# Convolutions beside the sampled steps, early scale constants, and a mixer start in another order, in a two-layer streaming encoder on one core

## The chip, the cores and the metric

One core of a Trainium2 chip. The metric is the device time of one execution in microseconds (us), the median over the runs shown. Of the core's engines TensorE (PE) does the matmuls, VectorE (DVE), ScalarE (ACT) and GpSimd (POOL) the rest, and SyncE (SP) issues most of the transfers.

## What is computed

One inference step of a two-layer encoder over 512 prompt tokens and 8 sampled sequences of 16 tokens, 640 tokens in all, 1024 wide, in fp32. Each layer is a SwiGLU, a mixer, and a second SwiGLU, each between two RMS norms with a modulation per sequence:

```python
h = _rmsnorm(x, norm_g[l, 2]) * (1.0 + sc2) + sh2
y, states = _token_mixer(h, l, layer_past, w_in, b_if, conv_w, conv_b, lam, ...)
x = x + g2 * _rmsnorm(y, norm_g[l, 3])
...
z = h @ w_in[l]                                   # 1024 -> 5640 columns
lmb = jnp.exp(jnp.sum(lp[0] * lp[1])) - jnp.exp(jnp.sum(lp[2] * lp[3])) + lam_init
...
a = p[:, :, 0] - lmb * p[:, :, 1]                 # differential attention, 4 heads
...
qk, conv_new = _causal_conv(z[..., OFF_MQ:OFF_MV], conv0, conv_w[l], conv_b[l])   # width 4, 1024 channels
qk = jax.nn.silu(qk)
...
hm, (c_new, n_new, m_new) = _mlstm(qm, km, vm, log_i, log_f, c0, n0, m0, blk)
merged = g[..., :D_MODEL] * (o_a @ w_pa[l]) + g[..., D_MODEL:] * (o_m @ w_pb[l])
```

The prompt attends within itself; every sampled sequence attends to 256 cached rows and its own 16. `z` feeds attention q, k, v, the memory's q and k (through the convolution), v, output gate, input and forget gates, and the two branch gates.

## The kernel before

Every fp32 matmul is made of three on reduced-precision parts (`three`; line 91 issues them, line 80 those into a PSUM bank that two tiles share): an operand is split into a high and a low part (`split`, lines 298 and 299; `split_to`, lines 504 and 505), the cast on ACT, the remainder on DVE or POOL. The 640 tokens are held transposed, as 8 groups of 128 channels, in two halves of 320 tokens.

A layer runs first FFN, mixer, second FFN. Large projections are computed in blocks (`blocks`, from line 740): a 2x2 block product with 7 products of 12 matmuls in place of 8. For it the token halves are combined (`combine`, lines 517 to 520: DVE and POOL alternate in place on the rows that `pre_norm` made, after they have been split) into t1 to t4, and the weight blocks are summed on POOL (lines 757, 758, 764, 771) before each sum is split on ACT and DVE (`split_to`, W tiles, four slots). A product lands in a PSUM tile (`acc`, four), from which DVE adds it into K tiles (line 747) or into the caller's `put` (line 887).

The mixer's order is written out in Python, and the program's scheduler moves instructions within what dependencies, buffers and its own estimates allow:

1. `attn_columns` (L876 in `first_columns`): q and k of heads 0 and 1, first for token half 0, then for token half 1; then `attn_values(0)`, which takes the values of both heads from five tiles of 128 tokens (`natural`, k0 in two slabs), and `head_rows`.
2. `side_blocks`: 14 blocks (q and k of heads 2 and 3, then the two branch gates, then the memory's q and k inputs, spilled to `pre` in DRAM), each interleaved through `zip_longest` with one part of the 16 prompt steps and 8 sampled steps of the attention. A sampled step loads 256 cached key rows (X tile), transposes them on PE (line 1110), scores (bank from X and S), takes a softmax on ACT and DVE (lines 1120 to 1132, `dm` and `sm` tiles), and multiplies with the cached values.
3. `history`, `values(0)`, `conv(0)`, `values(1)`, `conv(4)`. A `conv` call handles four groups of 128 channels: load the projection from `pre`, then on DVE a scale (line 1210), three multiply-adds (line 1212) each for the 512 prompt tokens (128x512) and for the sampled ones (128x128, from the tile `dm`, copied at line 1203), and a last multiply with the SiLU's tanh (line 1215).
4. `attention_out`, the memory's gates and chunks, the branches, the output projection.

At the mixer's start DVE also makes the scale constants from lambda: a load, two multiply-reduces (line 855), an Exp on ACT (857, with a table load), and five small operations (859 to 866, a memset on POOL among them).

SBUF tiles have few slots: W 4, X 3 (cached keys and, in the mixer's blocks, the sums s1 and s2 in one X tile), Fv 5, raw 4, C 8, S 42.

## Time and profile before

| | |
|---|---|
| median of 3 runs | 3140.17 us (3135.35 to 3141.33) |
| profiled execution, its own time | 3134.3 us |
| its span on the core | 3132.6 us |
| PE busy | 2989.2 us, 95% of the span |
| DVE busy | 2200.2 us, 70% |
| ACT, POOL busy | 1423.6 us, 1211.8 us |
| mean granted TensorE clock | 0.985 of 2.4 GHz |

How to read it: PE's busy time plus its idle time is the span, and an idle stretch of another engine costs nothing by itself. The granted clock is either 1 (2.4 GHz) or 0.5 (1.2 GHz); at 0.5 the same matmuls take twice as long, and that time counts as busy. The first mixer runs from about 553 to 1105 us, the second from about 2096 to 2655 us.

### The profile page before, as it was taken

What the parts mean: (1) busy time and instruction counts of PE and PEld (TensorE: products, weight loads), DVE (VectorE), ACT (ScalarE), POOL (GpSimd) and SP (SyncE); (2) the same over time, 40 slices, a digit from 0 to 9 for tenths busy, and PEclk for the clock granted to TensorE, in tenths of its full rate; (3) what the DMA queues carried; (4) which work ended last, traced back from release to release, by engine and by line L of the source; (5) the groups of instructions that cost most, each with busy time, mean ns of one, the idle gap of its engine ahead of it and who ended that gap; (6) DMA issues with size and microseconds to landing.
All of it is one profiled execution on the core that took longest, in us unless ns stands there. A gap on an engine that the chain in (4) does not pass through costs nothing. (4 is left out here: it accounts for less than half of the span.)

```text
span 3132.6 us, 51454 instructions
## 1 busy us (share of the span) xinstructions
PE 2989.2 (95%) x18765; PEld 2648.2 (85%) x18765; DVE 2200.2 (70%) x3959; ACT 1423.6 (45%) x2923; POOL 1211.8 (39%) x1119
## 2 busy tenths in 40 slices
PE   6999999898999989999999999998989999899998
PEld 5888877898898879998778888878989987899986
DVE  5776557677677678775676665667776866888755
ACT  5433346445434364444643333563553343644444
POOL 3574303343212166660255552134422122677502
PEclk9999999999999999999999999999999999999999
DMA  7555546234553553334555555461345445323345
GB/s 230 159 179 169 181 129 218 62 119 138 163 161 112 167 165 108 110 115 139 176 182 162 165 168 168 140 200 54 122 141 176 145 129 165 118 87 88 108 128 175
DMA packets 331680, 455.91 MB, mean 146 GB/s; under 512 B 24955, under 2 KB 223975, under 8 KB 331426
## 3 DMA queue, kind: packets, MB, share of 16 engines
q1 hardware_dynamic: 325778, 438.03, 45.0%
q0 software_dynamic: 5648, 14.57, 1.3%
q8 instruction: 149, 2.44, 0.3%
q14 instruction: 105, 0.86, 0.1%
HBM read 406.50 MB, written 46.02 MB: 144 GB/s over the span
## 5 line engine op out<-in xcount | busy, mean ns | idle before, releaser
L91 PE MATMUL acc<-S,W 128*128 128x320 f32 x3728 | 601.2, 312 | 6.6 <-DVE K L747 2.3
L91 PEld LDWEIGHTS acc<-S,W 128*128 128x128 f32 x3728 | 554.2, 188 | 55.4 <-ACT W L504 23.1
L299 DVE TENSOR_TENSOR W<-raw,W 128x1024 fp32r<-128x1024 f32 x242 | 308.7, 1276 | 273.0 <-ACT W L298 271.6
L91 PE MATMUL acc<-W,C 128*128 128x512 f32 x1848 | 443.9, 398 | 13.9 <-DVE W L299 7.0
L505 DVE TENSOR_TENSOR W<-raw,W 128x512 fp32r<-128x512 f32 (+1 forms) x384 | 327.7, 854 | 168.3 <-ACT W L504 153.1
L91 PEld LDWEIGHTS acc<-W,C 128*128 128x128 f32 x1848 | 342.8, 188 | 111.2 <-DVE W L299 17.1
L298 ACT CAST W<-raw 128x1024 fp32r<-128x1024 f32 x250 | 262.5, 1050 | 323.6 <-PE acc L91 200.7
L91 PE MATMUL acc<-C,W 128*128 128x320 f32 x2400 | 394.3, 315 | 10.2 <-ACT S L1002 6.4
L91 PEld LDWEIGHTS acc<-C,W 128*128 128x128 f32 x2400 | 363.4, 191 | 23.3 <-issue 9.8
L504 ACT CAST W<-raw 128x512 fp32r<-128x512 f32 (+1 forms) x384 | 236.6, 619 | 244.3 <-PE acc L91 141.8
L91 PE MATMUL bank<-S,X 128*128 128x320 f32 x1936 | 315.4, 310 | 0.0
L91 PEld LDWEIGHTS bank<-S,X 128*128 128x128 f32 x1936 | 291.6, 188 | 10.9 <-issue 8.4
L803 POOL TENSOR_TENSOR S<-S,K 128x320 f32<-128x320 f32 x160 | 174.5, 1108 | 242.4 <-DVE K L802 237.2
L505 POOL TENSOR_TENSOR C<-S,C 128x256 fp32r<-128x256 f32 x44 | 53.8, 1225 | 389.3 <-ACT C L504 389.1
L504 ACT CAST C<-S 128x384 fp32r<-128x384 f32 (+2 forms) x288 | 140.7, 498 | 137.9 <-PE acc L91 89.1
L91 PE MATMUL bank<-W,C 128*128 128x512 f32 x792 | 185.1, 395 | 0.0
L455 POOL TENSOR_TENSOR sm<-sm,mhalf 128x1 f32<-128x1 f32 (+2 forms) x80 | 63.9, 799 | 302.8 <-DVE sm L450 149.5
L505 DVE TENSOR_TENSOR X<-raw,X 128x512 fp32r<-128x512 f32 x160 | 161.8, 1012 | 25.0 <-ACT X L504 24.0
L91 PEld LDWEIGHTS bank<-W,C 128*128 128x128 f32 x792 | 148.7, 188 | 35.8
L764 POOL TENSOR_TENSOR raw<-raw 128x512 f32<-128x512 f32 x108 | 177.1, 1640 | 0.5
L757 POOL TENSOR_TENSOR Fa<-raw,raw 128x512 f32<-128x512 f32 x80 | 112.8, 1410 | 140.7 <-DMA raw<-in_w_ffn_dram 101.3
L91 PE MATMUL acc<-S,X 128*128 128x320 f32 x976 | 166.5, 312 | 0.0
(379 smaller groups left out, 5294.0 us busy)
## 6 DMA issues: line engine op xcount, KB each, us to landing
raw<-in_w_ffn_dram SPq DMA_DIRECT2D x348, 512.0 KB, 3.8
Fv<-in_w_ada_dram SPq DMA_DIRECT2D x261, 256.0 KB, 3.8
raw<-in_w_in_dram SPq DMA_DIRECT2D x72, 512.0 KB, 4.0
raw<-in_w_out_dram SPq DMA_DIRECT2D x32, 512.0 KB, 3.7
x<-X SPq DMA_DIRECT2D x25, 512.0 KB, 3.5
X<-x SPq DMA_DIRECT2D x25, 512.0 KB, 4.0
tanh<-K SPq DMA_DIRECT2D x64, 160.0 KB, 2.5
S<-tanh SPq DMA_DIRECT2D x32, 320.0 KB, 4.5
```

Source lines behind the costliest of these rows:

```text
L91: i = PE.matmul(out, lhsT, rhs, start=start, stop=stop).ins
L298: ACT.copy(hi, src)
L299: (eng or DVE).tensor_tensor(lo, src, hi.bitcast(F32), ALU.subtract)
L455: pows.append(POOL.tensor_tensor(r, t, mhalf.to_broadcast([P, n]), ALU.pow).ins)
L504: ACT.copy(hi, src)
L505: (eng or DVE).tensor_tensor(lo, src, hi.bitcast(F32), ALU.subtract)
L757: POOL.tensor_tensor(s1, a21, a22, ALU.add)
L764: POOL.tensor_tensor(a21, a11, a21, ALU.subtract)
L803: POOL.tensor_tensor(gm, gm, z, ALU.mult)
```

## The change

It moves the lambda constants of both layers into `late_constants`, which runs in the background of the first FFN; it takes the second token half's columns behind the first three value tiles of the first slab, with PSUM from `bank`; it takes the memory's q and k blocks ahead of the gates' blocks; it orders `combine` behind the last split on DVE of the half's rows; it holds s1 and s2 in two Fv tiles; it gives every channel group of a convolution its own tile for the sampled tokens, in place of `dm`; and it lets the convolutions advance beside the blocks and steps, from the 17th turn of that loop on, the rest behind `values(0)`.

```diff
@@ late_constants
+        for l in range(depth):
+            lam_init = 0.8 - 0.6 * math.exp(-0.3 * l)
+            lb = F("v")
+            load(lb[:, :256], lam[l].rearrange("a d -> (a d)").unsqueeze(0).to_broadcast([P, 256]))
+            sl = mk(per, [P, 8], "sl", depth)
+            le, nlm, cp, cs, na = sl[:, 0:2], sl[:, 2:3], sl[:, 3:5], sl[:, 5:6], sl[:, 6:7]
...
+            DVE.tensor_copy(cp[:, 0:1], one)
...
@@ split_to / combine
     def split_half(h, x, t):
         c = halves_of_tokens[t]
         for k in range(KD):
-            split_to(h[k, t], x[k][:, c], POOL if k % 4 == 3 else DVE)
+            i = split_to(h[k, t], x[k][:, c], POOL if k % 4 == 3 else DVE)
+            if k % 4 != 3:
+                last_split[:] = [i.name]
...
-            DVE.tensor_tensor(x1[:, a], x1[:, b], x1[:, a], ALU.subtract)
+            i = DVE.tensor_tensor(x1[:, a], x1[:, b], x1[:, a], ALU.subtract).ins
+            if hold:
+                in_order(i, last_split[0], "behind the split rows")
@@ blocks
-        if apart:
-            s12 = X((P, 2 * HK, P))
-            s1, s2 = s12[:, :HK], s12[:, HK:]
-        else:
-            s1, s2 = (F("a").rearrange("p (k c) -> p k c", k=HK) for _ in range(2))
+        s1, s2 = (F("v" if apart else "a").rearrange("p (k c) -> p k c", k=HK) for _ in range(2))
...
-                combine(*combinations.pop())
+                combine(*combinations.pop(), hold=apart)
@@ first_columns, side_blocks
-                    b = acc()[:, :TA]
+                    b = (bank if t else acc)()[:, :TA]
                     proj_t(b, w, h, t)
                     put(t, b)
+                yield
...
             parts = [(OFF_AQ + 256, keep(q, qscale)), (OFF_AK + 256, keep(k))]
+            parts += [(OFF_MQ + P * m, to_memory(pre, m)) for m in range(0, KD, 2)]
             parts += [(OFF_G + DM * br + P * m, to_memory(gate[br], m, half_tanh)) for br in range(2) for m in range(0, KD, 2)]
-            parts += [(OFF_MQ + P * m, to_memory(pre, m)) for m in range(0, KD, 2)]
@@ natural
+                orders = [range(3), range(3, NT)] if k0 == 0 else [range(NT)]
...
+                for tiles in orders:
+                    for kk in range(4):
+                        for i in tiles:
+                            kc = k0 + kk
+                            three(ys[i], htok(h, i)[kc], (wh[:, kk], wlo[:, kk]), kc == 0, kc == KD - 1)
+                    if k0 == 0 and tiles == orders[0]:
+                        between()
@@ conv
+                yield
-                z, zs = L((P, 3 + TOK)), once([P, 152], "dm").rearrange("p (b t) -> p b t", b=SB)
+                z, zs = L((P, 3 + TOK)), L()[:, :152].rearrange("p (b t) -> p b t", b=SB)
@@ mixer
-        attn_columns()
-        attn_values(0)
+        first = attn_columns()
+        next(first)
+        attn_values(0, lambda: next(first))
...
+        def convs():
+            for _ in range(16):
+                yield
+            history()
+            for base, dst, scale in ((0, qm, 0.5), (4, km, 0.5 * KSCALE)):
+                for _ in conv(base, dst, scale):
+                    for _ in range(2):
+                        yield
+
+        behind = convs()
         for _ in itertools.zip_longest(side, steps):
-            pass
-        history()
+            next(behind, None)
         _, _, tri = table(1)
         tri_b, mask_w, mask_wb, mask_t, mask_tb = table(2)
         values(0)
-        conv(0, qm, 0.5)
+        for _ in behind:
+            pass
         values(1)
-        conv(4, km, 0.5 * KSCALE)
         attention_out()
```

The work per engine stays as it was: PE has the same matmuls, 192 of which land in `bank` in place of `acc`, and POOL loses one memset per layer. On PE the order differs inside the two mixers only. Three places show how it moves; the line numbers in rows of the change are its own (523 there is 505 before, 539 is 517, 559 is 535, 580 is 556, 1118 is 1110, 1137 is 1129, 1219 and 1221 are 1210 and 1212).

PE at the start of the first mixer, before: the transposes of the last token tile's normed rows (`ident` with Fa and Fv) are followed by the columns of the second token half (acc from S and S).

```order
L91 MATMUL acc_5810<-S_4160,W_5504 128x320
L91 MATMUL acc_5810<-S_4161,W_5504 128x320
L535 MATMUL bank_5628<-ident_63,Fa_5605 128x128 x4
L91 MATMUL acc_5810<-S_4160,W_5505 128x320
L535 MATMUL bank_5639<-ident_63,Fv_5604 128x128 x4
L91 MATMUL acc_5837<-S_4146,S_5050 128x320
L91 MATMUL acc_5863<-S_4146,S_5274 128x320
L91 MATMUL acc_5837<-S_4147,S_5050 128x320
```

And with the change, 17 rows behind the second of those transposes (the rows between are of the first kind shown here):

```order
L80 MATMUL acc_5844<-W_5849,S_4175 128x256
L80 MATMUL acc_5844<-W_5849,S_4174 128x256
L80 MATMUL acc_5844<-W_5850,S_4174 128x256
L80 MATMUL acc_5844<-W_5849,S_4175 128x256
L80 MATMUL acc_5845<-W_5849,S_4168 128x256
L80 MATMUL acc_5845<-W_5850,S_4168 128x256
L91 MATMUL bank_5889<-S_4168,S_5072 128x320
L91 MATMUL bank_5915<-S_4168,S_5296 128x320
L91 MATMUL bank_5941<-S_4168,S_5432 128x320
L91 MATMUL bank_5967<-S_4168,W_5526 128x320
```

Between the transposes and the second half's columns (bank from S and S) there now stand the value tiles of token tiles 0 and 1 (acc from W and S, 128x256), which need the first half's rows only; some of the second half's columns are taken in between.

DVE at the same place, before: line 556 (behind 554) makes the last rows of h, 517 is `combine`, 505 the split of the second half.

```order
L556 TENSOR_TENSOR S_4140<-Fa_5633,shT_2695 128x128
L517 TENSOR_TENSOR S_4139<-S_4139 128x320
L556 TENSOR_TENSOR S_4142<-Fa_5644,shT_2695 128x128
L556 TENSOR_TENSOR S_4144<-Fa_5644,shT_2695 128x128
L517 TENSOR_TENSOR S_4138<-S_4138 128x320
L517 TENSOR_TENSOR S_4141<-S_4141 128x320
L505 TENSOR_TENSOR S_4149<-S_4139,S_4148 128x320
L517 TENSOR_TENSOR S_4140<-S_4140 128x320
L505 TENSOR_TENSOR S_4147<-S_4138,S_4146 128x320
L505 TENSOR_TENSOR S_4151<-S_4140,S_4150 128x320
L505 TENSOR_TENSOR S_4157<-S_4143,S_4156 128x320
L505 TENSOR_TENSOR S_4155<-S_4142,S_4154 128x320
```

With the change (523 splits, 539 combines):

```order
L580 TENSOR_TENSOR S_4160<-Fa_5655,shT_2717 128x128
L580 TENSOR_TENSOR S_4162<-Fa_5655,shT_2717 128x128
L578 TENSOR_TENSOR Fa_5666<-bank_5661,scT_2716 128x512
L523 TENSOR_TENSOR S_4169<-S_4160,S_4168 128x320
L523 TENSOR_TENSOR S_4171<-S_4161,S_4170 128x320
L580 TENSOR_TENSOR S_4164<-Fa_5666,shT_2717 128x128
L580 TENSOR_TENSOR S_4166<-Fa_5666,shT_2717 128x128
L523 TENSOR_TENSOR S_4173<-S_4162,S_4172 128x320
L523 TENSOR_TENSOR S_4179<-S_4165,S_4178 128x320
L523 TENSOR_TENSOR S_4177<-S_4164,S_4176 128x320
L523 TENSOR_TENSOR S_4181<-S_4166,S_4180 128x320
L539 TENSOR_TENSOR S_4160<-S_4160 128x320
```

All six splits now stand ahead of the first combination; the three small lambda operations that stood some rows above the first piece are gone from here.

PE at the first two sampled steps of the first mixer, before: transposes of cached keys (`ident` with X), the `dm` product that needs the softmax of the step, scores (bank from X).

```order
L91 MATMUL bank_8066<-S_5717,S_5719 32x128
L91 MATMUL bank_8066<-X_7959,S_5719 32x256
L91 MATMUL bank_8066<-S_5717,S_5719 32x128
L1110 MATMUL bank_8091<-ident_63,X_8088 128x128 x4
L1110 MATMUL bank_8097<-ident_63,X_8088 128x128 x4
L91 MATMUL bank_8170<-dm_8086,Fa_8075 128x128 x3
L91 MATMUL bank_8176<-X_8090,S_5718 32x256
L91 MATMUL bank_8176<-S_5717,S_5718 32x128
```

With the change, the end of what stands between the transposes of X_8088 and their step's `dm` product:

```order
L91 MATMUL acc_8402<-S_4196,W_8399 128x320
L91 MATMUL acc_8402<-S_4197,W_8399 128x320
L91 MATMUL acc_8402<-S_4196,W_8399 128x320
L91 MATMUL acc_8493<-C_4186,W_8490 128x320
L91 MATMUL acc_8493<-C_4187,W_8490 128x320
L91 MATMUL bank_8171<-dm_8086,Fa_8075 128x128 x3
L91 MATMUL bank_8177<-X_8090,S_5725 32x256
L91 MATMUL bank_8177<-S_5724,S_5725 32x128
```

Where before the `dm` product of the second step followed the transposes directly, now 45 matmuls of blocks (128x320) stand between the two; and between the transposes of the first step and these stand 36 rows, 24 of them block matmuls, where 12 stood.

DVE beside a later sampled step, before: 505 splits, 887 and 747 adds of block products, 1120 to 1132 the softmax of the step.

```order
L1125 TENSOR_TENSOR sm_8582<-sm_8579,slope_66 128x1
L1129 RECIPROCAL sm_8586<-sm_8584 128x1
L1130 TENSOR_TENSOR sm_8586<-sm_8586,cs_5681 128x1
L1111 COPY X_8593<-bank_8600 128x512
L1132 TENSOR_SCALAR dm_8589<-S_5666,sm_8586 128x128
L505 TENSOR_TENSOR W_8651<-X_8610,W_8651 128x512
L887 TENSOR_TENSOR K_8647<-K_8613,acc_8634 128x320
L505 TENSOR_TENSOR W_8739<-raw_8606,W_8739 128x512
L505 TENSOR_TENSOR W_8757<-X_8610,W_8757 128x512
```

With the change, beside the step of the same kind (771 is 747 before):

```order
L1219 TENSOR_SCALAR S_8770<-S_8762,cwb_5735 128x512
L1219 TENSOR_SCALAR S_8770<-S_8763,cwb_5735 128x128
L1221 SCALAR_TENSOR_TENSOR S_8770<-S_8762,cwb_5735,S_8770 128x512
L771 TENSOR_TENSOR K_8797<-K_8635,acc_8784 128x320
L1221 SCALAR_TENSOR_TENSOR S_8770<-S_8763,cwb_5735,S_8770 128x128
L1137 RECIPROCAL sm_8607<-sm_8605 128x1
L1119 COPY X_8614<-bank_8621 128x512
L523 TENSOR_TENSOR W_8928<-raw_8919,W_8928 128x512
L1221 SCALAR_TENSOR_TENSOR S_8770<-S_8762,cwb_5735,S_8770 128x512
L1221 SCALAR_TENSOR_TENSOR S_8770<-S_8763,cwb_5735,S_8770 128x128
L1138 TENSOR_TENSOR sm_8607<-sm_8607,sl_1754 128x1
```

The scale and the multiply-adds of one group of channels (1219, 1221) now stand between the step's and the blocks' operations. The piece of DVE's order that holds the first three groups whole is 84 operations long: those 30, 16 splits, 16 adds of products and 22 smaller ones; PE's order has 200 block matmuls and 62 others from that piece's first split to its last, and POOL's 11 block sums. The five other groups stand behind `values(0)`.

## Rows read from the trace of the kernel before

**Rows 1.** page part 1, busy time, share of the span and instructions of each engine

```profile
PE 2989.2 (95%) x18765; PEld 2648.2 (85%) x18765; DVE 2200.2 (70%) x3959; ACT 1423.6 (45%) x2923; POOL 1211.8 (39%) x1119
```

**Rows 2.** windows of stretches: length, busy PE, PEld, DVE, ACT, POOL, clock, DMA, GB/s

```profile
560.00:600.00 40.00, 31.84 (x212) 30.71 (x211) 26.43 (x49) 15.60 (x34) 15.49 (x21) 0.87 0.13 44
772.00:790.00 18.00, 10.63 (x89) 8.51 (x90) 10.76 (x24) 7.58 (x21) 6.59 (x6) 0.81 0.41 117
790.00:895.00 105.00, 105.00 (x900) 97.03 (x900) 63.17 (x137) 39.62 (x89) 25.44 (x25) 1.00 0.56 174
895.00:935.00 40.00, 36.75 (x302) 36.23 (x302) 39.04 (x96) 14.38 (x32) 6.21 (x20) 0.99 0.54 175
2104.00:2145.00 41.00, 32.02 (x205) 30.73 (x205) 25.85 (x47) 15.65 (x34) 15.46 (x21) 0.83 0.13 42
2317.00:2336.00 19.00, 11.56 (x106) 9.19 (x105) 10.88 (x25) 7.35 (x22) 6.58 (x6) 0.82 0.36 112
```

**Rows 3.** PE timeline, start of the first mixer: start, duration, row, [idle before]

```profile
578.70 7.47 PE L91 MATMUL acc<-S,S 128*128 128x320 f32 x38 [4.09 <-DVE S L505]
```

**Rows 4.** windows of PE at the lower clock: length, PE busy, granted clock, DMA

```profile
572.10:582.40 10.30, 4.74 (x18) 0.50 0.01 2
780.30:787.10 6.80, 3.40 (x24) 0.50 0.35 101
2114.90:2128.60 13.70, 7.35 (x26) 0.50 0.00 0
```

**Rows 5.** DVE timeline, start of the first mixer

```profile
564.83 0.23 DVE L855 CUSTOM_DVE_ANT_0 Fv<-Fv 128x64 f32<-128x64 f32 x1 [1.45 <-DMA Fv<-in_lam_dram]
...
576.04 0.48 DVE L505 TENSOR_TENSOR S<-S,S 128x320 fp32r<-128x320 f32 x1
...
577.51 4.79 DVE L505 TENSOR_TENSOR S<-S,S 128x320 fp32r<-128x320 f32 x5
```

**Rows 6.** PE timeline, first sampled steps of the first mixer

```profile
778.51 1.07 PE L1110 MATMUL bank<-ident,X 128*128 128x128 f32 x8 [2.59 <-DMA X<-in_cache_k_dram]
783.70 1.62 PE L91 MATMUL bank<-dm,Fa 128*128 128x128 f32 x6 [4.12 <-DVE dm L1132]
...
790.55 3.69 PE L91 MATMUL acc<-C,W 128*128 128x320 f32 x24
```

**Rows 7.** DVE timeline, the same steps and the stretch behind them

```profile
780.69 2.54 DVE L1130 TENSOR_TENSOR sm<-sm,cs 128x1 f32<-128x1 f32 x1
...
804.81 1.79 DVE L505 TENSOR_TENSOR W<-X,W 128x512 fp32r<-128x512 f32 x1
```

**Rows 8.** POOL timeline beside the first of these two

```profile
781.95 1.26 POOL L771 TENSOR_TENSOR raw<-raw,X 128x512 f32<-128x512 f32 x1
```

**Rows 9.** DVE groups by line and shape, 895 to 985 us, convolutions: count, busy, mean ns

```profile
L1212 DVE SCALAR_TENSOR_TENSOR S<-S,cwb,S 128x512 f32<-128x512 f32 x24 | 17.7, 751 | 0.0
...
L1212 DVE SCALAR_TENSOR_TENSOR S<-dm,cwb,S 128x128 f32<-128x128 f32 x24 | 8.4, 348 | 0.1
...
L1215 DVE SCALAR_TENSOR_TENSOR S<-S,S 128x640 f32<-128x640 f32 x8 | 6.6, 819 | 0.0
L1210 DVE TENSOR_SCALAR S<-S,cwb 128x512 f32<-128x512 f32 x8 | 4.4, 546 | 1.0 <-DMA S<-pre 1.0
...
L1210 DVE TENSOR_SCALAR S<-dm,cwb 128x128 f32<-128x128 f32 x8 | 2.7, 342 | 0.0
...
L1203 DVE COPY dm<-S 128x128 f32<-128x128 f32 x8 | 1.8, 227 | 0.2
```

**Rows 10.** DVE groups by line and shape, 790 to 895 us, sampled steps beside blocks

```profile
L505 DVE TENSOR_TENSOR W<-raw,W 128x512 fp32r<-128x512 f32 x22 | 16.9, 767 | 0.9 <-ACT W L504 0.8
L505 DVE TENSOR_TENSOR W<-X,W 128x512 fp32r<-128x512 f32 x8 | 10.4, 1303 | 3.9 <-ACT W L504 3.9
L887 DVE TENSOR_TENSOR K<-K,acc 128x320 f32<-128x320 f32 x19 | 9.2, 485 | 6.7 <-PE acc L91 6.5
L747 DVE TENSOR_TENSOR K<-K,acc 128x320 f32<-128x320 f32 x15 | 7.3, 485 | 4.4 <-PE acc L91 4.4
```

More of the change, by code (lines that the diff above doesn't have):

```diff
@@ L222 @@
     tables = []
+    scales = []
     def table_parts(j, t):
@@ L289, in late_constants @@
         DVE.tensor_tensor(comb.rearrange("p (h r) -> p h r", h=NH)[:, :, :ST], eq[:, 0], eq[:, 1], ALU.add)
+        for l in range(depth):
[4 more added lines that the diff above has]
+            le, nlm, cp, cs, na = sl[:, 0:2], sl[:, 2:3], sl[:, 3:5], sl[:, 5:6], sl[:, 6:7]
+            for e in range(2):
+                DVE.tensor_tensor_reduce(out=lb[:, 256:320], in0=lb[:, 128 * e:128 * e + 64], in1=lb[:, 128 * e + 64:128 * e + 128],
+                                         scale=1.0, scalar=0.0, op0=ALU.mult, op1=ALU.add, accum_out=le[:, e:e + 1])
+            ACT.activation(le, le, AF.Exp)
+            DVE.scalar_tensor_tensor(nlm, le[:, 1:2], -lam_init, le[:, 0:1], ALU.add, ALU.subtract)
+            DVE.tensor_copy(cp[:, 0:1], one)
+            DVE.tensor_copy(cp[:, 1:2], nlm)
+            DVE.scalar_tensor_tensor(cs, c01[:, 1:2], nlm, c01[:, 0:1], ALU.mult, ALU.add)
+            DVE.tensor_scalar(na, nam[:, l:l + 1], 1.0 - lam_init, None, ALU.mult)
+            scales.append((cp, cs, na))
         for j, (t, n) in enumerate(zip(ts, (TOK, PAST + 240 + P, TOK))):
@@ L848, in once @@
             return mk(per, shape, tag, bufs)
-        lb = F("v")
-        load(lb[:, :256], lam[l].rearrange("a d -> (a d)").unsqueeze(0).to_broadcast([P, 256]))
-        le = once([P, 2], "le")
-        for e in range(2):
-            DVE.tensor_tensor_reduce(out=lb[:, 256:320], in0=lb[:, 128 * e:128 * e + 64], in1=lb[:, 128 * e + 64:128 * e + 128],
-                                     scale=1.0, scalar=0.0, op0=ALU.mult, op1=ALU.add, accum_out=le[:, e:e + 1])
-        ACT.activation(le, le, AF.Exp)
-        nlm = once([P, 1], "nlm")
-        DVE.scalar_tensor_tensor(nlm, le[:, 1:2], -lam_init, le[:, 0:1], ALU.add, ALU.subtract)
-        cp = once([P, 2], "cp")
-        POOL.memset(cp[:, 0:1], 1.0)
-        DVE.tensor_copy(cp[:, 1:2], nlm)
-        cs = once([P, 1], "cs")
-        DVE.scalar_tensor_tensor(cs, c01[:, 1:2], nlm, c01[:, 0:1], ALU.mult, ALU.add)
-        na = once([P, 1], "na")
-        DVE.tensor_scalar(na, nam[:, l:l + 1], 1.0 - lam_init, None, ALU.mult)
+        cp, cs, na = scales[l]
         nm = nam[:, depth + l:depth + l + 1]
@@ L970, in keep, with attn_values @@
                 return put
-            first_columns([keep(q, m, qscale[m]) for m in range(2)] + [keep(k, m, 1.0) for m in range(2)])
-        def attn_values(hp):
+            return first_columns([keep(q, m, qscale[m]) for m in range(2)] + [keep(k, m, 1.0) for m in range(2)])
+        def attn_values(hp, between=lambda: None):
             ys = halves()
-            natural([(OFF_AV + 256 * hp, 256)], 256, ys)
+            natural([(OFF_AV + 256 * hp, 256)], 256, ys, between)
             for i in range(NT):
```

12 lines of the change are left out of this document (4 added, 8 removed).

## The prediction

> **What bounds the kernel now.** I read the page's busy times first. PE is busy for 2989.2 of 3132.6 us [rows 1]; no other engine is near. The matmuls stay the same in number and shape, so the change can win only what PE idles, 3132.6 - 2989.2 = 143 us in the whole program, and what PE loses at its lower clock. On PE the order changes inside the mixers alone, so I then read windows of the mixers' stages [rows 2]; the reader should compare a window's length with PE's busy time. The first mixer's start idles 40.00 - 31.84 = 8.2 us, the second's 41.00 - 32.02 = 9.0; the first sampled steps idle 18.00 - 10.63 = 7.4 us and 19.00 - 11.56 = 7.4. The stretch behind them, 790 to 895 us, idles not at all, with DVE busy for 63.17 of 105. The stretch of the convolutions, 895 to 935 us, idles 3.25 us, and there DVE is busy for 39.04 of 40: the one place where DVE is full.
>
> Third, the waits themselves on PE's timeline. At the mixer's start the longest is 4.09 us for a split of the second token half [rows 3]. At the sampled steps there are two: 2.59 us for a cached key tile and 4.12 us for `dm`, the end of a softmax [rows 6]. Fourth, the clock. Behind each of these idle times the granted clock is 0.50, 1.2 GHz [rows 4], and the PE busy time in those windows would be half at 2.4 GHz: the price is 4.74 / 2 = 2.4 us at the first mixer's start, 7.35 / 2 = 3.7 at the second's, 3.40 / 2 = 1.7 at the sampled steps. So the price of the starts is 8.2 + 2.4 = 10.6 and 9.0 + 3.7 = 12.7 us, that of the sampled steps 7.4 + 1.7 = 9.1 us in each layer (the second layer's clock taken as the first's).
>
> **Mixer start.** Three edits act here together. (a) Lambda leaves: on DVE the wait of 1.45 us for its load stands in front of the residual's last rows [rows 5], and the small operations and the Exp behind it go too. They run in the first FFN's background, where PE waits for none of them; a load, some ten short DVE operations and an Exp per layer, at the 0.23 us of the row, are under 3 us of DVE, which is busy for 70% [rows 1]; PE keeps on with blocks there. I cost them at nothing; without that cover they would cost 3 us a layer once. The removed POOL memset is off PE's path. (b) `combine` goes behind the splits. Before, five splits took 4.79 us, 0.96 each, beside POOL's part of `combine`, where one alone took 0.48 [rows 5]; four DVE subtractions stood among them. Now the six splits come first. What is late next is t13 and t42, which the first block needs only after the value tiles of 5 x 24 matmuls and more. (c) PE gets 26 or more value matmuls of 128x256 from the first half ahead of the second half's columns, and more among these. At the mean of the busy stretch, 105 us / 900 = 0.117 us a matmul [rows 2], 26 are 3.0 us. With DVE ahead by 1.45 us and by about 5 x 0.48 = 2.4, this covers 6.9 us of the 8.2 in the first layer. I take 1.2 us of waiting as left in either layer and the clock as kept, since the two long waits are gone: -9.4 and -11.5 us. Bounds: all gone (-10.6, -12.7), or only the 3.0 us of filler (-3.0 each).
>
> **Sampled steps.** The `dm` wait of 4.12 us now has 45 block matmuls of 128x320 on PE: at 3.69 / 24 = 0.154 us each [rows 6], 6.9 us. The X wait of 2.59 has 24 of them, 3.7 us, and X no longer holds s1 and s2, so the keys' load can start earlier. Both are covered. I leave 1.1 us for the first step, which is not: -8.0 a layer. Bounds -9.1 and -4.0 (the softmax chain slower beside blocks, below). The Exp table is now loaded by the first prompt step; PE has blocks there, so nothing.
>
> **Convolutions beside the sampled steps: the new cost.** One group of channels costs DVE (17.7 + 8.4 + 6.6 + 4.4 + 2.7 + 1.8) / 8 = 5.2 us [rows 9]. Three of eight move into a piece of 84 DVE operations. I cost it by rows of the stretch that holds the same work [rows 10]: 12 splits from raw at 0.767 = 9.2, 4 from the sums at 1.303 = 5.2, 16 adds at 0.485 = 7.8, three groups 15.6; the 22 small ones by that stretch's remainder, (63.17 - 16.9 - 10.4 - 9.2 - 7.3) / 105 = 0.185 us per us of PE. PE has 200 x 0.154 + 62 x 0.117 = 38.1 us in it, so the small ones are 7.0 and DVE needs 44.8 us: 6.7 more than PE. DVE may run ahead by some of the four W slots: a product of 12 is 1.85 us, two slots 3.7, four 7.4. By this alone PE waits between 0 and 3 us, where it waited for nothing.
>
> A second price comes on top. On DVE's timeline a 128x1 operation that reads two SBUF tiles took 2.54 us [rows 7]: it began at 780.69 and ended when POOL's block sum did, at 781.95 + 1.26 = 783.21 [rows 8]. That is most of the 4.12 us wait. A split beside another sum took 1.79 us against a mean of 0.767, +1.0 us. In the piece POOL has 11 sums. If DVE, now full, meets each, it loses 11 x 1.0, less the 4 x (1.303 - 0.767) = 2.1 already counted: +8.9 more. The adds read only one SBUF tile, and at 0.485 their two groups show no such cost.
>
> The Trainium skill's page "SBUF — State Buffer", section "Who interferes with whom", states the rule that speaks against this change: a VectorE instruction with two SBUF inputs and a GpSimd one that reads SBUF exclude each other, whoever is second waiting for the whole of the first. The 2.54 us row agrees. By the rule in full, every multiply-add of a convolution that meets a sum waits, and the piece would cost PE the upper end below.
>
> So the new wait is between 0 (four slots of lead) and 6.7 + 8.9 - 3.7 = 11.9 us a layer; I take 5, a little under the middle, since many of the 22 sums and adds stand between multiply-adds, and those scales, copies and adds do not collide. SP's loads from `pre` now stand among the cached values' loads; DVE's longest idle before a load of `pre` was 1.0 us over eight [rows 9], inside that range.
>
> **Values.** Five groups instead of eight now run behind `values(0)`, but all five ahead of the copies of `values(2)`. Between the split that opens the piece and the first such copy DVE had 25.6 us of convolutions by the rows' means and now has 24.5: 1.1 us less, in a stretch where PE idles 3.25 and DVE is full [rows 2]. I take 0; bounds -3 and +4 (the multiply-adds that used to come later bunched before one copy).
>
> **Sum.** Starts -9.4 - 11.5 = -20.9; sampled steps -16.0; convolutions +10.0; values 0: -26.9 us. From the profiled execution's 3134.3 that is 3107.4. It stood 5.9 us under the median of the runs shown, 3140.17; on the median's scale I forecast 3113 us. A measurement of this kernel tells about 0.2%, 6.3 us, from no change, so faster is under 3133.9, slower over 3146.4.
>
> **Rivals.** (1) DVE's lead hides the convolutions: 3140.2 - 36.9 = 3103. For it: DVE has 42 us of idle in the 105 before, and all four W slots may be ahead. Against: 44.8 against 38.1. (2) DVE becomes the bound beside the sampled steps: +11.9 twice, 3140.2 - 36.9 + 23.8 = 3127. For it the 2.54 and 1.79 us rows. (3) The start does not move as the order says: DVE ends the splits as late as now because the residual's chain, not `combine`, sets them, and only the 3.0 us of filler count: 20.9 - 6.0 = 14.9 us lost of the gain, 3128. For it: the lambda wait is partly the slack of a chain through POOL and ACT. Against: the 4.79 us row. (4) Slower: case 2, and its waits bring the clock down. At the sampled steps 2.59 and 4.12 us of idling were followed by 6.8 us at 0.50 [rows 4, 6]. If in each layer the 38 us of the piece run at 1.2 GHz for half their length, 19 us, 9.5 us more are lost per layer, 3127 + 19 = 3146, with 3 us more from the bunched values 3149. It turns the sign once over 6.6 us a layer are lost to the clock, 13 us at 0.50. Against it: waits of 1 or 2 us between products, not of 4.
>
> **Chances.** Forecast 0.48, rival (1) 0.20, (2) 0.15, (3) 0.10, (4) 0.07. Faster: the first two wholly, most of (2) and (3), whose errors of some 6 us reach into no change: 0.84. Same 0.09, slower 0.07. The range leaves out the lower end of (1) and the upper of (4): 3097 to 3136.
>
> **What would show it.** In the profile after: windows of the mixer starts with PE idle under 2 us and the clock at 1; the `dm` product with no wait; DVE near full beside the sampled steps with multiply-adds of 1.5 us or more beside POOL's sums, and PE waits on DVE W there of 3 to 7 us a layer; the values stretch as before. The forecast is wrong if PE waits at the starts for over 4 us, if that piece costs none or over 12, or if a stretch of 10 us there stands at 0.50.

## The result, and the profile after

The changed kernel takes 3090.64 us (median of 4 runs, 3084.05 to 3091.88) against 3139.51 before (4 runs, 3135.35 to 3141.33): a ratio of 0.9842, with an interval of 0.9825 to 0.9859. That is 49 us faster, where 27 were forecast, and below the range's lower end of 3097. The two profiled executions lie closer together, since that of before was among its fastest runs and that of the change the slowest of its four: spans of 3132.6 and 3090.1 us, 42.5 apart. The terms below are held against these 42.5. One run each of e8 and e16 below, at a clock of 0.31 and 0.65, is left out of their medians.

First the changed kernel's page, busy time of each engine: PE has lost 11.7 us of busy time without losing a matmul, and its idle time is down from 143.4 to 112.6 us [rows 1]. The clock is the smaller part of the 11.7: in all stretches at 0.50 together PE is busy for 62.8 us before and for 57.4 after, and half of that difference, 2.7 us, is what the clock gave back. The other 9 us are matmuls that follow each other faster outside these stretches, a gain that shows as no wait before the change.

```profile
PE 2977.5 (96%) x18765; PEld 2646.3 (86%) x18765; DVE 2189.9 (71%) x3961; ACT 1423.2 (46%) x2925; POOL 1207.4 (39%) x1117
```

Then windows of the stages, to be read against [rows 2]: length, busy time of PE, PEld, DVE, ACT and POOL, granted clock, DMA share and GB/s.

```profile
560.00:600.00 40.00, 40.00 (x303) 39.64 (x302) 33.34 (x51) 17.92 (x39) 26.66 (x30) 1.00 0.17 58
757.00:790.00 33.00, 31.54 (x271) 29.67 (x269) 25.04 (x57) 17.98 (x44) 10.16 (x9) 1.00 0.66 207
802.40:845.40 43.00, 40.51 (x332) 37.15 (x327) 38.65 (x85) 20.87 (x45) 12.48 (x19) 1.00 0.64 199
880.00:920.00 40.00, 39.21 (x316) 38.82 (x315) 38.68 (x118) 16.51 (x33) 5.04 (x17) 1.00 0.48 160
2075.00:2125.00 50.00, 49.91 (x367) 49.01 (x368) 42.12 (x70) 24.13 (x56) 28.84 (x33) 1.00 0.18 60
```

Both mixer starts (the first and last row) are full, at a clock of 1.00: 8.2 and 9.0 us of idling and two spells at 0.50 are gone (in the second layer 0.1 us of idling is left). The first sampled steps, in the second row, still idle 1.5 us. The third row is the piece in which the first three groups of the convolutions now lie: PE idles 2.5 us there, and DVE is busy for 38.65 of 43. In the stretch behind `values(0)` (the fourth row) PE idles 0.8 us where it idled 3.25, though DVE is as full as before.

The waits on PE's timeline that answer to [rows 3, 6]: start, duration, row, and in brackets the idle time ahead of it.

```profile
772.56 1.06 PE L1118 MATMUL bank<-ident,X 128*128 128x128 f32 x8 [1.46 <-DMA X<-in_cache_k_dram]
...
835.85 1.99 PE L91 MATMUL acc<-S,W 128*128 128x320 f32 x12 [1.41 <-DVE K L771]
838.76 3.49 PE L91 MATMUL acc<-S,W 128*128 128x320 f32 x22 [0.91 <-ACT K L780]
...
894.88 4.02 PE L80 MATMUL acc<-W,S 128*128 128x256 f32 x32 [0.79 <-ACT S L1010]
```

Of the waits at the sampled steps the one for `dm` is gone and that for a key tile is 1.46 us (2.90 in the second layer, there with a spell at 0.50). In place of the `dm` wait stand the block matmuls of the new order, directly ahead of the product:

```profile
773.38 6.53 PE L91 MATMUL acc<-S,W 128*128 128x320 f32 x43
779.74 0.46 PE L91 MATMUL acc<-C,W 128*128 128x320 f32 x2
780.03 0.83 PE L91 MATMUL bank<-dm,Fa 128*128 128x128 f32 x6
```

The two waits of 1.41 and 0.91 us are new, beside the convolutions. The last, 0.79 us, is the only one left in the values stretch; the wait of before there (below) is gone.

How much earlier the n-th matmul of the program starts than before, read at the stages' borders (PE's order differs inside the mixers, so borders inside one are good to about 1 us):

| stage | forecast, both layers | first layer | second layer |
|---|---|---|---|
| mixer start | -20.9 | -11.6 | -13.9 |
| blocks up to the sampled steps | 0 | -2.7 | -1.6 |
| first sampled steps | -16.0 | -7.1 | -5.2 |
| blocks beside the convolutions | +10.0 | +0.6 | +1.3 |
| values and first branch columns | 0 | -4.0 | -3.2 |
| all else | 0 | +5.1 in sum | |

"All else" is the kernel's start (+2.0) and the first FFN of the second layer with the weights of its modulation (+3.1). In the other kernels below the start stands between 0 and 3.5 us whether lambda is made early or late (7.0 in e12, which has fewer S slots), so it belongs to the executions and not to the change. The second stands between 0.7 and 2.9 us in them (10 in e12) and was not explained.

### The profile page after: what moved, and what is told of

It reads as the page before. It is cut to its first block, busy times and chain, and to the rows that moved or that the text cites. A ratio compares the mean times of both kernels' runs of the same rounds, so it can differ in the third digit from the quotient of the medians.

```text
span 3090.1 us, 51438 instructions
## 1 busy us (share of the span) xinstructions
PE 2977.5 (96%) x18765; PEld 2646.3 (86%) x18765; DVE 2189.9 (71%) x3961; ACT 1423.2 (46%) x2925; POOL 1207.4 (39%) x1117
## 4 chain that ended last, share of the span: by engine, by line
PE 83%; DVE 6%; DMA 6%; ACT 2%; issue 2%; POOL 1%; SPq 0%; DVEq 0%; POOLq 0%; ACTq 0%
PE acc L91 48%; PE bank L91 30%; PE acc L80 3%; DMA raw<-in_w_ffn_dram 2%; DVE W L317 1%; DMA S<-tanh 1%; ACT W L316 1%; DVE S L1221 1%; DMA S<-pre 1%; DMA S<-in_w_ada_dram 1%; DVE S L523 0%; PE bank L1118 0%; PE bank L559 0%; DMA Fv<-in_w_ada_dram 0%; SPq L114 0%
## 5 line engine op out<-in xcount | busy, mean ns | idle before, releaser
L91 PEld LDWEIGHTS acc<-S,W 128*128 128x128 f32 x3680 | 549.3, 189 | 58.6 <-ACT W L522 26.2
L91 PE MATMUL acc<-W,C 128*128 128x512 f32 x1848 | 444.9, 398 | 15.3 <-DVE W L317 9.1
L523 DVE TENSOR_TENSOR W<-raw,W 128x512 fp32r<-128x512 f32 (+1 forms) x384 | 320.7, 836 | 162.2 <-ACT W L522 157.0
L91 PEld LDWEIGHTS acc<-C,W 128*128 128x128 f32 x2400 | 360.3, 190 | 13.9 <-issue 7.8
L91 PEld LDWEIGHTS acc<-S,X 128*128 128x128 f32 x976 | 148.3, 188 | 17.7 <-issue 10.9
```

The costliest lines, as they stand in the source:

```text
L91: i = PE.matmul(out, lhsT, rhs, start=start, stop=stop).ins
L523: return (eng or DVE).tensor_tensor(lo, src, hi.bitcast(F32), ALU.subtract).ins
```

## The experiments

All times are medians; each job ran the kernel before on the same chip, at 3138.75 to 3139.81 us.

**The convolutions' place.** First everything but that (e1).

```diff
         for _ in itertools.zip_longest(side, steps):
-            next(behind, None)
+            pass
+        history()
...
         values(0)
-        for _ in behind:
+        for _ in conv(0, qm, 0.5):
             pass
         values(1)
+        for _ in conv(4, km, 0.5 * KSCALE):
+            pass
```

> All of the change but the convolutions' place: history and values(0) first, then conv(0), values(1), conv(4), as before the change. Theory A (the convolutions beside the steps cost little there, about 1.5 us a layer, and give more back behind values(0)): slower than the changed kernel by 4 to 12 us, about 3098; in the values stretch DVE full and PE waiting about 3 us for an ACT copy again, with a spell at 0.50. Rival B (they cost the 5 us a layer that was forecast, and the gain comes from elsewhere): faster than the changed kernel by 5 to 10 us, about 3083.

Measured: 3089.08 us (ratio to before 0.9843, 0.9828 to 0.9859), no difference from the changed kernel, so neither total came true. The stages have the signs of theory A, but a price nearer to rival B's. Its stretch behind `values(0)` on PE's timeline:

```profile
907.64 1.97 PE L1241 MATMUL bank<-ident,r 128*128 128x128 f32 x8 [3.20 <-DVE C L1180]
910.71 6.89 PE L91 MATMUL acc<-C,W 128*128 128x320 f32 x36 [1.10 <-ACT S L1010]
918.30 6.90 PE L91 MATMUL acc<-C,W 128*128 128x320 f32 x45 [0.70 <-DVE S L1504]
```

The waits are back (3.20, 1.10, 0.70) and by windows a mean clock of 0.91 from 890 to 930 us; from 800 to 845 us PE idles not at all. By stages the new place costs 3.8 and 3.6 us beside the steps (theory A had 1.5 a layer, rival B 5) and gives back 7.0 and 5.6 behind `values(0)`. So against before, the stage beside the steps is 3.2 and 2.3 us shorter in e1, where no convolution stands in it: what the other edits gain there. In the memory heads of the second layer this kernel is 9.5 us quicker than the changed one, so that the sum is nil. What that last is was not settled, so the nil of the totals is not accounted for by these two stages alone; the one other kernel with slot, start, blocks' order and late convolutions (e14, below) shows 6.8 us of it.

Two other places, both with lambda made late (neutral, see below). First half of the groups beside the steps and half behind `values(1)` (e15):

```diff
-            for base, dst, scale in ((0, qm, 0.5), (4, km, 0.5 * KSCALE)):
-                for _ in conv(base, dst, scale):
-                    for _ in range(2):
-                        yield
+            for _ in conv(0, qm, 0.5):
+                for _ in range(2):
+                    yield
...
         values(1)
+        for _ in conv(4, km, 0.5 * KSCALE):
+            pass
```

> The changed kernel with lambda at the mixer's start and only conv(0)'s four groups beside the steps and behind values(0), conv(4) behind values(1) as before. If five groups ahead of values(2) are what still costs 2 us there: 3080 to 3086. If the stretch is even: 3086 to 3092.

Measured 3094.56 us (0.9856, 0.9841 to 0.9870): above both ranges, not better than the changed kernel, a little worse if anything.

Then all of them, six turns of the loop earlier (e18):

```diff
-            for _ in range(16):
+            for _ in range(10):
                 yield
```

> The changed kernel with lambda at the mixer's start and the convolutions allowed from the 11th turn on instead of the 17th. If DVE has room there (36 of 43 us busy behind, less ahead): more groups beside the steps, none left to bunch, 3080 to 3086. If they meet POOL's sums and the loads of their inputs: 3090 to 3100 with PE waits beside the steps.

Measured 3115.97 us (0.9926, 0.9912 to 0.9939): 25 us slower than the changed kernel and above both ranges. Here DVE does become the bound. In the window of the first sampled steps and in the next 40 us of that kernel:

```profile
757.00:790.00 33.00, 27.27 (x167) 25.11 (x166) 32.97 (x65) 15.19 (x32) 13.21 (x22) 0.95 0.44 129
790.00:830.00 40.00, 34.09 (x247) 31.52 (x248) 38.47 (x77) 18.93 (x42) 14.19 (x19) 0.91 0.59 176
```

DVE is busy for 32.97 of 33 us and PE for 27.27, and the clock is 0.95 and 0.91. So DVE does bound PE when the convolutions may start ten turns into the loop; at sixteen their place costs the 3.8 and 3.6 us of e1.

**The sums' slot.** The change without it (e5), and it without the change (e13). The edit of e5 is this; e13 is the same lines the other way round, in the kernel before.

```diff
-        s1, s2 = (F("v" if apart else "a").rearrange("p (k c) -> p k c", k=HK) for _ in range(2))
+        if apart:
+            s12 = X((P, 2 * HK, P))
+            s1, s2 = s12[:, :HK], s12[:, HK:]
+        else:
+            s1, s2 = (F("a").rearrange("p (k c) -> p k c", k=HK) for _ in range(2))
```

> All of the change, with the blocks' sums s1 and s2 again in one X tile. In this kernel's order on PE the second sampled step's dm product again follows the transposes of its keys directly. Theory C (the sums' slot in X is what kept block matmuls and cached keys from overlapping): the waits of about 2.6 us for a key tile and 4.1 us for dm return with a spell at 0.50; slower than the changed kernel by 12 to 18 us, about 3106; the mixer starts and the values stretch as in the changed kernel. Rival D (the convolutions and blocks moved beside the steps fill them whatever the slots): no such waits, slower by 0 to 4 us.

Measured 3119.27 us (0.9937, 0.9922 to 0.9951), 28.6 us slower than the changed kernel: theory C, and by more than it said. The waits at the sampled steps are the old ones, and two more, of 2.02 and 2.90 us, stand beside the convolutions:

```profile
767.10 1.64 PE L1122 MATMUL bank<-ident,X 128*128 128x128 f32 x8 [2.68 <-DMA X<-in_cache_k_dram]
772.20 1.62 PE L91 MATMUL bank<-dm,Fa 128*128 128x128 f32 x6 [3.46 <-DVE dm L1144]
...
820.86 2.61 PE L91 MATMUL acc<-S,W 128*128 128x320 f32 x12 [2.02 <-DVE W L523]
...
845.26 1.00 PE L91 MATMUL bank<-dm,Fa 128*128 128x128 f32 x6 [2.90 <-DVE dm L1144]
```

By stages it is 6.9 and 4.4 us at the sampled steps and 6.2 and 6.3 in the piece beside the convolutions. So with the sums in X the new place of the convolutions costs more than was forecast, 6.8 and 7.6 us against before (e16 below, with the sums in X and the convolutions at their old place, neither gains nor loses there).

> The kernel before with one edit: the blocks' sums s1 and s2 in two Fv tiles instead of one X tile. Its order on PE has the block matmuls between the keys' transposes and the dm product as the changed kernel has. Theory C (the slot alone brings the sampled steps' gain): first sampled steps without the 2.6 and 4.1 us waits, 7 to 9 us a layer less; 14 to 22 us faster than before, about 3120; the mixer starts as before. Rival (the slot needs the convolutions' new place or the blocks' order too): 0 to 6 us faster.

Measured 3111.31 us (0.9914, 0.9899 to 0.9928): 27.6 us faster than before by this edit alone, over half of the whole gain: theory C, and by more than it said. The starts, which were to stay as before, gain 2.9 and 7.2 us. The windows of the sampled steps and of the stretch behind them in that kernel:

```profile
757.00:790.00 33.00, 32.98 (x251) 30.91 (x251) 25.45 (x58) 18.54 (x47) 13.92 (x11) 1.00 0.53 164
790.00:880.00 90.00, 90.00 (x808) 83.31 (x808) 51.30 (x125) 32.72 (x74) 15.19 (x18) 1.00 0.60 185
```

PE is idle for 0.02 of 33 us. In the second layer the `dm` wait is gone too, but one of 2.61 us for a key tile remains. Is it the free slot for the keys? The next kernel (e12) is the changed one with the sums in X and a fourth X tile, at the price of two S slots.

```diff
-        return shaped(mk(per, [P, 1032], "X", 3, dt), shape)
+        return shaped(mk(per, [P, 1032], "X", 4, dt), shape)
...
-        return shaped(mk(per, [P, 645], "S", 42), shape)
+        return shaped(mk(per, [P, 645], "S", 40), shape)
```

> The changed kernel with the sums back in an X tile, but four X slots instead of three (two of the 42 S slots given up for the room). PE's order at the first sampled steps is that of the kernel before. Theory C1 (a free slot for the keys is what counts): the wait for the key tile, 2.6 us, is gone or under 1; the dm wait stays, since nothing stands between; 3108 to 3116. Rival C2 (what counts is the order that the slots let the scheduler write): both waits stay, 3117 to 3122.

Measured 3148.13 us (1.0028, 1.0016 to 1.0040): 28.9 us slower than e5, from which it differs by the slots alone, so the total says nothing of the keys' slot. The waits do:

```profile
780.01 1.07 PE L1122 MATMUL bank<-ident,X 128*128 128x128 f32 x8 [2.89 <-DMA X<-in_cache_k_dram]
784.90 1.62 PE L91 MATMUL bank<-dm,Fa 128*128 128x128 f32 x6 [3.82 <-DVE dm L1144]
```

Both are there with a fourth slot, as rival C2 had it. What goes with the gain is the order: with s1 and s2 outside X the scheduler puts 43 (e13) or 45 (the changed kernel) block matmuls between a step's transposes and its `dm` product, and in e12 it puts none. That a fourth X tile with all 42 S slots would not bring that order too is not shown.

**The mixer's start.** Three edits, taken away one by one, two by two, and all. The windows from 560 to 600 us, the first mixer's start, give PE's idle time (8.2 before, 0.0 with the change):

| kernel | lambda early | combine behind the splits | value tiles between | PE idle, us | median, us |
|---|---|---|---|---|---|
| changed (and once more) | yes | yes | yes | 0.0 | 3090.64, 3088.22 |
| e3 | no | yes | yes | 0.05 | 3086.11 |
| e4 | yes | no | yes | 0.6 | 3091.17 |
| e2 | yes | yes | no | 1.8 | 3095.50 |
| e8 | no | yes | no | 2.5 | 3098.03 |
| e9 | yes | no | no | 4.2 | 3102.45 |
| e6 | no | no | no | 4.9 | 3105.48 |

The intervals of these medians are 8 to 13 us wide, that of e2 23 (0.9844 to 0.9917), so the totals of e2, e3 and e4 are not clearly apart from the changed kernel's. The edits are the parts of the diff, undone: for `combine` and the value tiles this, and for lambda its block put back to the mixer's start, with `once` for its columns as before. What was expected of e2, e3, e4, e6, e8, e9 and of the changed kernel once more stands behind the edit, in this order.

```diff
-            combine(*combinations.pop(), hold=apart)
+            combine(*combinations.pop())
...
-                    b = (bank if t else acc)()[:, :TA]
+                    b = acc()[:, :TA]
...
-                orders = [range(3), range(3, NT)] if k0 == 0 else [range(NT)]
+                orders = [range(NT)]
...
-        attn_values(0, lambda: next(first))
+        next(first)
+        attn_values(0)
```

> All of the change but the tiles' order at the mixer's start: both halves' columns first, PSUM from acc, then the value tiles in one piece. Lambda stays early and combine stays behind the splits. Theory A (PE lacked work there; the value tiles fill it): slower than the changed kernel by 8 to 20 us, about 3104, with PE waits of 4 to 6 us for splits at each start and a spell at 0.50. Rival B (lambda and combine held the splits up, and with both gone they are in time): slower by 0 to 5 us, about 3093.

> All of the change, with lambda's constants made at each mixer's start as before. Theory A (tile order does most): slower by 1 to 5 us, about 3094, by a DVE wait of 1 to 2 us for the load that PE's value tiles cover. Rival B (the load's wait and the Exp set the chain): slower by 8 to 16 us.

> All of the change, without the order of combine behind the last split. Theory A: slower by 0 to 6 us, about 3093: splits of 0.9 to 1 us beside POOL's half of combine, PE waits of 1 to 2 us at each start, no spell at 0.50. Rival B (combine was the delay): slower by 8 to 16 us, with a spell at 0.50 at each start.

> All of the change but what acts at the mixer's start: lambda back there, combine free, both halves' columns ahead of the value tiles. Theory E (the three edits cover the same waiting, and any two are nearly enough): the start idles 8 to 9 us again with a spell at 0.50, slower than the changed kernel by 22 to 28 us, about 3115. Rival F (something else in the change, slots or the blocks' order, gives part of it): the start idles 3 to 6 us, slower by 8 to 16 us.

> Of the three edits at the mixer's start only combine behind the splits; lambda at the mixer's start, both halves' columns ahead of the value tiles. Theory E (combine's half on DVE is what delays the splits by 4 us; lambda's load is 1.5 us): start idle 3.5 to 5.5 us, slower than the changed kernel by 7 to 14 us, about 3100. Rival G (lambda's load, at the head of the chain, delays everything): start idle 6 us and more, slower by 15 us and more.

> Of the three edits at the mixer's start only lambda's early constants; combine free, both halves' columns ahead of the value tiles. Theory E: start idle 6 to 7.5 us and a spell at 0.50, slower than the changed kernel by 18 to 24 us, about 3111. Rival G (lambda's load delays everything): start idle 3 to 5 us, slower by 8 to 12 us.

> The changed kernel once more, beside the others on the same chip: 3085 to 3092. Lambda's place counts if the kernels with lambda at the mixer's start are under it by more than the intervals; nothing expected there, 0 to 4 us.

e4 came as theory A had it. e2 went to its rival's side: with lambda and combine gone the splits are nearly in time. e3 fell out of both: with the other two edits in, lambda's place does nothing to the total that can be measured (without the value tiles' order it is worth 0.7 us of idling, e2 against e8 and e9 against e6). e6 went to its rival: without any of the three the start idles 4.9 us, not 8, so another part of the change gives the rest, and e13 shows which, since with the slot alone the same window idles 4.8. e8 came as theory E in time (7.4 us slower) with less idling than it had; e9 lies in the ranges of rival G (4.2 us idle, 11.8 slower), though not by its reason, since e6, with lambda late, idles only 0.7 us more. The wait in e6 answers to [rows 3]:

```profile
577.85 1.97 PE L91 MATMUL acc<-S,S 128*128 128x320 f32 x6 [4.16 <-DVE S L507]
```

and on DVE the subtractions of combine (523 in that kernel) stand ahead of the splits (507) again:

```profile
573.97 2.77 DVE L523 TENSOR_TENSOR S<-S 128x320 f32<-128x320 f32 x4
576.66 1.14 DVE L507 TENSOR_TENSOR S<-S,S 128x320 fp32r<-128x320 f32 x1
...
578.79 4.14 DVE L507 TENSOR_TENSOR S<-S,S 128x320 fp32r<-128x320 f32 x5
```

Five splits take 4.14 us there; in the changed kernel, ahead of the subtractions, four (523 in it) take 2.37:

```profile
574.54 2.37 DVE L523 TENSOR_TENSOR S<-S,S 128x320 fp32r<-128x320 f32 x4
576.83 3.07 DVE L539 TENSOR_TENSOR S<-S 128x320 f32<-128x320 f32 x4
```

**What the parts need of each other.** The start's edits and the blocks' order, without slot and convolutions (e16, whose edit is those of e1 and e5 together); and slot and start without the blocks' order and the convolutions (e17, the edit of e1 and this):

```diff
             parts = [(OFF_AQ + 256, keep(q, qscale)), (OFF_AK + 256, keep(k))]
-            parts += [(OFF_MQ + P * m, to_memory(pre, m)) for m in range(0, KD, 2)]
             parts += [(OFF_G + DM * br + P * m, to_memory(gate[br], m, half_tanh)) for br in range(2) for m in range(0, KD, 2)]
+            parts += [(OFF_MQ + P * m, to_memory(pre, m)) for m in range(0, KD, 2)]
```

> The changed kernel with the convolutions' place and the sums' X tile as before; the three edits at the mixer's start and the memory's blocks ahead of the gates' stay. Theory H (beside the steps the convolutions cost 5 us and more a layer only while the sums hold an X tile, and the start's edits give 20 to 25 us): about 3116, faster than the kernel with the sums in X and the convolutions beside the steps by 0 to 8 us. Rival (the convolutions cost the same either way, near nothing): 3119, the same as that kernel.

Measured 3124.10 us (0.9956, 0.9942 to 0.9970), above both. The starts gain 11.6 and 13.4 us against before, all that the changed kernel gains there, and the values stretch gives back 7.6 and 6.5.

> The changed kernel with the convolutions behind values(0) and values(1) and the memory's blocks behind the gates', both as before: the start's edits and the sums' slot are left. Theory I (the blocks' order alone costs in the values stretch, and is there for the convolutions): PE waits of 3 us there as in the kernel before instead of 4.5, 3086 to 3092. Rival (the order gains by itself): 3093 to 3100.

Measured 3109.32 us (0.9905, 0.9892 to 0.9919), above both: 20 us slower than with the memory's blocks first (e1). The start's edits add only 2 us to the slot here, no more than the noise: against e13 they gain some 7 us at each start, and the values stretch gives 9.6 and 7.0 back, in waits for DVE's C tiles and ACT's copies:

```profile
911.66 1.12 PE L1241 MATMUL bank<-ident,r 128*128 128x128 f32 x4 [1.97 <-DVE C L1180]
914.15 1.11 PE L1241 MATMUL bank<-ident,r 128*128 128x128 f32 x4 [1.38 <-DVE C L1180]
916.50 3.57 PE L91 MATMUL acc<-C,W 128*128 128x320 f32 x12 [1.24 <-ACT S L1010]
922.89 7.40 PE L91 MATMUL acc<-C,W 128*128 128x320 f32 x31 [2.82 <-ACT S L1010]
```

So the blocks' order, which I had not priced at all, is worth 20 us once slot and start are in. Why is open. With their blocks last, the convolutions' loads from `pre` might come late, but DVE's wait for such a load is 1.0 us in e17 and 0.6 in e1, so this is not where 20 us lie. In the first layer e17 is 4.8 us behind e1 ahead of the values stretch and loses 4.6 more in it, where DVE is busy for 40.0 of 40 us (890 to 930) in both.

e1's edit and e3's together (e14):

> The changed kernel with two edits undone that by themselves changed the time by less than 5 us: lambda at the mixer's start and the convolutions behind values(0) and values(1). If both are neutral: 3087 to 3092, no difference from the changed kernel. If the two small gains add: 3080 to 3086, faster than the changed kernel by 5 to 10 us.

Measured 3091.43 us (0.9849, 0.9835 to 0.9864): both edits neutral. No version was found that is faster than the changed kernel by more than the intervals.

## Why the prediction was wrong

**The convolutions' move, +10.0 beside the steps and 0 in the values stretch, is the step that failed most.** Against before, these two stages give -5.3 us (+1.9 and -7.2) where the sum has +10.0: 15.3 of the 15.6 us that the sum fell short. Held against e1, the move itself costs 7.4 us beside the steps, so the size of that cost was nearly right, and brings 12.6 in the values stretch, which was put at 0. The other edits bring 5.5 beside the steps and cost 5.4 in the values stretch. That PE did not idle beside the steps before the change and yet 5.5 us were won there, and 4.3 in the blocks ahead of them, goes against the first step of my reasoning, that only idle time and the clock can be won. In e1's total the move does not show, since the 9.5 us of the second layer's memory heads stand against it.

That the 5 us a layer came near to the measured 3.8 and 3.6 is in part luck, since both of its sources were misread. I had held a sum of 44.8 us of DVE rows against 38.1 of PE. The groups of the changed kernel in that piece, DVE by line and shape, count, busy us and mean ns, the dearest five:

```profile
L523 DVE TENSOR_TENSOR W<-raw,W 128x512 fp32r<-128x512 f32 x12 | 8.7, 724 | 0.2 <-ACT W L522 0.2
L1221 DVE SCALAR_TENSOR_TENSOR S<-S,cwb,S 128x512 f32<-128x512 f32 x9 | 7.7, 856 | 0.0
L1221 DVE SCALAR_TENSOR_TENSOR S<-S,cwb,S 128x128 f32<-128x128 f32 x9 | 4.0, 442 | 0.0
L771 DVE TENSOR_TENSOR K<-K,acc 128x320 f32<-128x320 f32 x8 | 3.8, 480 | 1.0 <-PE acc L91 1.0
L891 DVE TENSOR_TENSOR K<-K,acc 128x320 f32<-128x320 f32 x8 | 3.8, 477 | 0.7 <-DMA tanh<-K 0.7
```

With the smaller groups they add up to 45.4 us, close to what I had; but the window above has DVE busy for 38.65. The difference, 6.8 us over 85 operations, is 0.08 us each: when DVE works without a pause, a row begins 0.08 us before the one ahead of it ends (77 of that window's rows do, by 0.08 us in the mean). Two rows of the changed kernel's DVE timeline show it, the first ending at 837.28 + 0.34 = 837.62:

```profile
837.28 0.34 DVE L1221 SCALAR_TENSOR_TENSOR S<-S,cwb,S 128x128 f32<-128x128 f32 x1
837.54 0.81 DVE L1224 SCALAR_TENSOR_TENSOR S<-S,S 128x640 f32<-128x640 f32 x1
```

Durations of rows, added up, are not the time that an engine needs for them. A busy time of a window is nearer to it, and by that DVE is the shorter of the two: 38.65 to 40.51 of PE. So DVE was not the bound there; PE's 2.5 us of idling in the piece are single waits.

The second source, POOL's sums in DVE's way, was right in kind and too large by its count. In the changed kernel a multiply-add that takes 0.75 us alone takes 1.78 beside a sum, and POOL's sum 1.74 where others take 1.28:

```profile
811.27 1.25 DVE L1221 SCALAR_TENSOR_TENSOR S<-S,cwb,S 128x128 f32<-128x128 f32 x1
...
813.11 1.18 DVE L523 TENSOR_TENSOR W<-raw,W 128x512 fp32r<-128x512 f32 x1
814.21 1.78 DVE L1221 SCALAR_TENSOR_TENSOR S<-S,cwb,S 128x512 f32<-128x512 f32 x1
```

```profile
811.09 1.28 POOL L777 TENSOR_TENSOR Fv<-raw,raw 128x512 f32<-128x512 f32 x1 [0.98 <-DMA raw<-in_w_in_dram]
812.45 1.29 POOL L778 TENSOR_TENSOR Fv<-Fv,raw 128x512 f32<-128x512 f32 x1
813.70 1.74 POOL L784 TENSOR_TENSOR raw<-raw 128x512 f32<-128x512 f32 x1
...
819.14 1.34 POOL L791 TENSOR_TENSOR raw<-raw,Fv 128x512 f32<-128x512 f32 x1 [0.64 <-DVE W L523]
...
835.47 1.27 POOL L791 TENSOR_TENSOR raw<-raw,Fv 128x512 f32<-128x512 f32 x1 [10.89 <-DVE W L523]
```

But only these five sums fall into the piece, not the 11 that I counted from POOL's order: POOL had run the others ahead. The four splits of the sums take 0.68 us in the piece, not the 1.30 of the row that I priced them by [rows 10]; this is not the tile's place, since in e5, with the sums in X, seven of them took 0.82 beside the convolutions. The rule of the Trainium skill ("SBUF — State Buffer", section "Who interferes with whom") that whoever is second waits agrees with these rows. The split of 813.11 begins while the sum of 812.45 runs and ends 0.55 us after it (814.29 against 813.74), the next sum ends 1.15 us after that split (815.44), and the multiply-add of 814.21 ends 0.55 us after that sum (815.99): as it would be if each row held a wait for the one before. I had written that scales, copies and adds do not collide; against that, a scalar operation of 128x128 (line 1140) took 1.36 us at 819.25 while the sum of 819.14 ran, where the two others of the piece took 0.28. All this decides little here, since DVE had the time.

**The values, taken as 0, gained 7.2.** I had counted DVE's convolutions up to the first copy of `values(2)`, 25.6 and 24.5 us. PE waited for the last copy. Before, on DVE (line 1001) and PE:

```profile
928.06 0.49 DVE L1001 COPY S<-acc 128x128 f32<-128x128 f32 x2
...
933.51 0.49 DVE L1001 COPY S<-acc 128x128 f32<-128x128 f32 x2
...
934.17 8.43 PE L91 MATMUL acc<-C,W 128*128 128x320 f32 x46 [2.90 <-ACT S L1002]
```

With the change (line 1009), and no wait at PE's products behind them:

```profile
907.30 0.29 DVE L1009 COPY S<-acc 128x128 f32<-128x128 f32 x1
...
911.79 0.49 DVE L1009 COPY S<-acc 128x128 f32<-128x128 f32 x2
```

Behind the piece's first split (894.13 and 875.24) the first copies come after 33.9 and 32.1 us, the last ones after 39.4 and 36.6. Up to the last ones the convolutions' rows on DVE are 27.6 us before and 26.2 now, half of these 2.8 us; the other half was not traced to a row. What it was worth to PE can be added up: 3.25 us of idling and a spell at 0.50 behind it in which PE was busy for 3.13 us, 1.6 of them due to the clock, against 0.79 us now, makes the -4.0 of the first layer. My bounds of -3 and +4 a layer missed it, as they had no term for the clock.

**The sampled steps were priced for the right place and for half of the reason.** -12.3 of -16.0: `dm` is covered, as forecast, but of the key tile's wait, which the sum had as covered, 1.46 and 2.90 us remain. What covers `dm` is the order that comes with the slot (e13, e5). The slot's work elsewhere, 2.9 and 7.2 us at the starts and 2.0 and 0.9 in the blocks behind the steps (e13's stages), I had not seen, so that the single edit that carries over half of the gain stood in the sum as a share of one term. The blocks' order, worth 20 us between e17 and e1, had no term at all.

**The starts were right** in their mechanism, -25.5 of -20.9, the waits gone altogether and 2.2 us beyond the bound of -23.3; e16, without the slot, has the same gain there (25.0). Of the three edits lambda, which I had put first, does next to nothing, and combine with the tiles nearly all of it. **Rival (1)**, at 3103 with a chance of 0.20, came nearest. Rival (2) describes what six turns earlier do (e18: 3116, with DVE as the bound), though its sum has 3127.

## What to carry to other kernels

Hold a stretch's work on an engine against the time there by the busy time of windows, not by adding up rows' durations; and count what an engine must have done up to the last result that the waiting engine needs. An edit that gives two users of a buffer pool tiles of their own can be worth more than its wait in the profile, here where it changed the order that the scheduler wrote. A stretch in which PE never idles can still get shorter. Gains at one stage may be given back at the next that is full, so what a part of a change is worth depends on the others: here the same three edits at the start were worth 2 us beside the slot alone (e17 against e13) and 15 beside all the rest (e6).

## What had not been expected of the hardware

Rows of consecutive DVE operations overlap by 0.08 us (45.4 us of rows in 38.65 us). Where DVE's and POOL's rows overlap on SBUF both get longer, the sum 1.74 us instead of 1.28 and the multiply-add 1.78 instead of 0.75; before the change a 128x1 operation had shown the same with 2.54 us [rows 7]. The TensorE clock stayed at 1.00 through the waits of 1.41 and 0.91 us beside the convolutions and fell to 0.50 in the second layer behind the wait of 2.90, and in e1 at the same place behind one of 1.81 us.
